# A one-core decoder step: a rotation's second half, a sample's start and a weight load move along the stream of input projections

## The chip, the cores and the metric

The kernel runs on one core of a Trainium2 chip. Its time is the device time of one execution in microseconds; shorter is better. TensorE (PE) multiplies matrices, VectorE (DVE) and ScalarE (ACT) work element by element, GpSimd (POOL) does a little of that and issues DMAs, SyncE (SP) only issues DMAs. Each takes its instructions in a fixed order and waits on semaphores for the others.

## The reference

One inference step of a single decoder layer, for a prompt of 1024 tokens and 8 samples of 4 tokens, all in float32 with D_MODEL 1024. Cut to what matters here:

```python
xn = rms_norm(x, g_pre_mix)
h = xn @ w_in            # [q_a|k_a|v_a|q_r|k_r|v_r|gate_r|gm_a|gm_r], 5888 columns
qr = rope_ret(q_r); kr = rope_ret(k_r) * DK_R ** -0.5
   # rope_ret(x) = x * cos + rot * sin, rot = stack([-x[1::2], x[0::2]])
o_r, new_s = retention(qr, kr, v_r, state)       # 4 heads, chunks of 128 tokens
y_a = o_a @ w_a_proj
y_r = (silu(gate_r) * head_rms(o_r)) @ w_r_proj
x = x + rms_norm((sigmoid(gm_a) * y_a + sigmoid(gm_r) * y_r) @ w_o, g_post_mix)
x = x + rms_norm(conv_ffn(rms_norm(x, g_pre_ffn)), g_post_ffn)
```

The samples use the same layer, with a retention state for each of the 8 (state_ret) that is read, used and written back.

## The kernel before

Precision: each float32 operand is split into a high part (a rounding cast, ScalarE) and the rest (a subtraction, VectorE); a product is three matmuls, high by high, high by low, low by high (lines 255 to 257, in mm3).

The large products are done with seven block products instead of eight, by sums of blocks of the weights and of the activations. The names A11, A12, A22, S1 to S4 stand for these seven products, and for their splits of the weights.

The part that the change touches is the function stream. It computes 16 groups of two 128-column blocks of w_in: first four pairs of q_r and k_r (one for each head), then the ret_gate, the gm_a and the gm_r columns. Each group is done for two halves of the 1056 tokens (i is the group, j the half). A half is seven products of 12 matmuls each (128x264 outputs), in the order A11, S1, A22 of the half before, S2, A12, S4, S3. They gather in PSUM banks: A11 and A12 in the one named q0, S2, S3 and A22 in q1 (two buffers), S1 and S4 in q2. The results go to a tile named pair by copies (L927) and two additions: L950 adds bank q2, after S4, and L952 adds bank q1, after S3. S1 of the next half writes q2, so it waits for L950.

stream is a generator, and every product is a yield: adv(n) runs n products and leaves the rest for later, so that other work (the samples, the retention blocks) is written between products.

The weights of the group after are prepared by in_split, a generator too. It loads two raw tiles (w_raw, L819, issued by SP, 512 KB each), and then gives one split after another; each is a cast on ACT (L331) and a subtraction on DVE (L223, where nearly all of DVE's two-operand work is recorded, in the helper ew). One split needs a sum of both halves of the second raw tile (s1, out<-in "s<-w_raw"). While the samples run there are two buffers for raw tiles; behind them a third is added.

For q_r and k_r a rotation follows each half (post_qk). In its first step the neighbouring rows of pair are exchanged by four DMAs on SP into two tiles sh (L860). The second step, turned, does three DVE operations for each of q and k (pair times rcos, sh times rsin, their sum) and stores the result to qk_d (L868, POOL). The first step is run by flush, at S2 of the half after; the second is kept in the list LATER and taken from there.

The samples (the function sample, once for each of 4 heads) begin after adv(20). A sample loads its rotated q and k from qk_d (L1045, SP), copies them (L1050, ACT), multiplies them (L1057), masks (L1060, DVE) and splits them (L1063, L1064). Then, four times, two retention states are split (s0s; L228 on ACT, L223 on DVE), multiplied (L1078), and updated (L1083 on PE, L1084 on DVE), and the new state is stored (L1086, POOL). At the end comes a norm over DVE (L1090), ACT (L1017, L1019, L1022) and POOL (L1021), and two transposes (L1028). s0s has one buffer, the raw states four.

The kernel is written with a framework that orders the instructions itself: a scheduler takes those that are ready by its own estimate of times, and prefers what the program has earlier. So a line that moves in the program can change the order of all engines around it. Semaphores and waits come from the framework.

Of the kernel before, what the change touches and what calls it, by code (L numbers as in the profile page):

```python
# [107 lines left out]
A11, A12, A22, S1, S2, S3, S4 = range(7)  # L108
# [12 lines left out]
def trunk(ctx, tc, I, O):  # L121
# [49 lines left out]
    def TT(name, shape=(P, T), dt=F32):  # L171
        return tpool.tile(list(shape), dt, name=name, tag="T")
# [17 lines left out]
    def psum(pl, tag, dt=F32):  # L190
        return pl.tile([P, 512], dt, name="ps_" + tag, tag=tag)
# [598 lines left out]
    ORDER = [0, 1, 2, 3, 4, 5, 8, 6, 9, 7, 10, 11, 12, 13, 14, 15]  # L790
# [108 lines left out]
    PEND, LATER = [], []  # L899

    def stream():

        ws = in_split(ORDER[0])
        next(ws)
        next(ws)
        ops = {p: next(ws) for p in EARLY[:5]}
        coming = in_split(ORDER[1])
        next(coming)
        last, nh = None, 0
        for i, n in enumerate(ORDER):  # L910
            for j in range(2):
                o = TT("pair")
                c11, c12, c21, c22 = (o[:, HW * q:HW * q + HW] for q in range(4))
                dst = {A12: c11, S1: c22, S2: c12, A22: c21}
                bk = [psum(pq, "q%d" % b)[:, :HW] for b in (0, 2)]
                b1 = pq.tile([P, 512], F32, name="ps_q1", tag="q1", bufs=2)[:, :HW]
                bk.insert(1, b1)
                if j:
                    nxt = {}

                def product(p, ps, t, j, dst):
                    for k in range(4):
                        xh, xl = xop(ex1, p, j, k)
                        mm3(ps, t[:, k], t[:, 4 + k], xh, xl, p in (A11, S1) and k == 0, k == 3,
                            skip_group_check=p not in (A11, S1))
                    if p in dst:
                        S.copy(out=dst[p], in_=ps)  # L927

                for p in (A11, S1, A22, S2, A12, S4, S3):
                    if p == A22:  # L930
                        if last is not None:
                            product(A22, *last)
                        if j == 0 and i:
                            ops[A22] = next(ws)
                            ws = coming
                            if i + 1 < len(ORDER):
                                next(ws)
                        if last is not None:
                            yield
                        continue  # L940
                    if p == S2:
                        if nh < 2:
                            TE.matmul(bk[1], ops[p][:, 0], xop(ex1, p, j, 0)[0], start=True, stop=True)
                            S.copy(out=bk[1], in_=bk[0])
                        nh += 1
                    product(p, bk[{A11: 0, A12: 0, S2: 1, S3: 1, S1: 2, S4: 2}[p]], ops[p], j, dst)
                    if p == A11 and nh >= 2:
                        S.copy(out=bk[1], in_=bk[0])
                    if p == S4:
                        V.tensor_tensor(out=c12, in0=bk[2], in1=c12, op=add)  # L950
                    if p == S3:
                        V.tensor_tensor(out=c22, in0=bk[1], in1=c22, op=add)  # L952
                    if p == S2:
                        flush()
                    if p == S1 and LATER:
                        LATER.pop()()
                    if p == S4 and S3 not in ops:
                        ops[S3] = next(ws)
                    if p == S3 and A22 not in ops:
                        ops[A22] = next(ws)  # L960
                        ws = coming
                        next(ws)
                    if j and i + 1 < len(ORDER):
                        nxt[p] = next(ws)
                        if p == S4 and i + 2 < len(ORDER):
                            coming = in_split(ORDER[i + 2])
                            next(coming)
                    yield
                last = bk[1], ops[A22], j, dst
                PEND.append(POST[n](j, o))  # L970
            if i + 1 < len(ORDER):
                ops = nxt
        product(A22, *last)
        flush()
        yield
# [3 lines left out]
    def adv(n):  # L979
        for _ in range(n):  # L980
            next(STR, None)

    def flush():
        while PEND:
            PEND.pop(0)()
# [108 lines left out]
    turns = []  # L1094
    for n in range(2):
        load_s0(n)
    adv(20)
    for h in range(4):
        for n, _ in enumerate(sample(h)):
            adv(3 if n < 4 else 2)  # L1100
# [30 lines left out]
    zlast, gts, qks, vts, state, quads, NBLK = [], {}, {}, {}, {}, {}, 4 * NB  # L1131
# [117 lines left out]
    coming, behind = ahead(0), None  # L1249
    for g in range(NBLK):  # L1250
        f, coming = coming, ahead(g + 1)
# [8 lines left out]
        behind = (g,) + m  # L1260
    adv(1)
    tail(*behind)
    adv(len(ORDER) * 14 - 8 - 82 - 4 * NBLK - 1)
    for n in range(4):
        load_z(n, quarters(ST("zt", (P, T), bufs=3)) if n < 2 else TT("z_raw", (P, 4, HW)))
    for _ in STR:
# [459 lines left out]
    ws = [products(S4, 1, pt, (1,), (0,)) for pt in range(3)]  # L1726
# [63 lines left out]
```

## Time and profile before

| | us |
|---|---|
| median of 3 runs | 1656.74 (1656.53 to 1758.46) |
| the profiled execution, its own time | 1658.69 |
| its span | 1656.9 |
| PE busy | 1626.7 |
| DVE busy | 1205.9 |
| ACT busy | 863.6 |
| POOL busy | 446.3 |

The profile is of one execution. Its times count from the first instruction. A row of a timeline is start, duration, engine, line, operation, out<-in, and in brackets the idle time of the engine before it and what ended that. In an entry of the waits, "PE ps_q L255 <- DVE pair L950: 3.1, 2, 2.1" means that PE waited at line 255, writing ps_q, for VectorE's instruction of line 950: 3.1 us in total, 2 times, 2.1 us the longest. The buffer numbers are left out in the profile's names. A matmul's record overlaps the next one; in an undisturbed stretch one starts every 0.12 us.

### The profile page before, as it was taken

Reading aid. Unit: us, or ns where it says so; the run is one execution under the profiler, and the core shown is the slowest. Engines: PE = TensorE matmul, PEld = TensorE weight load, DVE = VectorE, ACT = ScalarE, POOL = GpSimd, SP = SyncE. Lnnn points to the kernel's source line nnn. Section 1 sums busy time; section 2 is a strip of 40 time slices with the busy share of each in tenths; the row PEclk is TensorE's granted clock in tenths of the full one; section 3 lists DMA queues with packets and bytes.
Section 4 is the critical chain, followed back from the end, with each engine's and each line's share of the span. In section 5 each row is a group of like instructions: output and inputs, shape, how many; then the busy total and the mean of one; then the engine's idle time right before and its main releaser. Section 6 shows DMA issues by size and latency. Waiting matters only on the chain.

```text
span 1656.9 us, 32509 instructions
## 1 busy us (share of the span) xinstructions
PE 1626.7 (98%) x12551; PEld 1589.6 (96%) x12551; DVE 1205.9 (73%) x2035; ACT 863.6 (52%) x1882; POOL 446.3 (27%) x654
## 2 busy tenths in 40 slices
PE   8999999999999999999999999999999999999997
PEld 7999999999999999999789999999999999999997
DVE  7878749688565655569748988988988988445476
ACT  6565634456565655564424655555555556443343
POOL 4232431012233332243312422321231322111111
PEclk9999999999999999999999999999999999999999
DMA  7212235556677665697422245454545548766664
GB/s 201 65 49 71 72 80 193 185 187 191 207 230 235 197 216 156 209 309 234 157 89 89 59 148 173 161 162 160 182 136 177 173 150 253 237 196 198 194 186 145
DMA packets 275852, 278.22 MB, mean 168 GB/s; under 512 B 23552, under 2 KB 234784, under 8 KB 275681
## 3 DMA queue, kind: packets, MB, share of 16 engines
q1 hardware_dynamic: 241937, 159.58, 33.2%
q0 software_dynamic: 33760, 116.57, 20.1%
q8 instruction: 98, 1.61, 0.4%
q14 instruction: 57, 0.47, 0.1%
HBM read 184.24 MB, written 87.49 MB: 164 GB/s over the span
## 4 chain that ended last, share of the span: by engine, by line
PE 71%; DMA 3%; DVE 1%; issue 1%; ACT 0%; POOL 0%; DVEq 0%; POOLq 0%; SPq 0%
PE ps_m L255 10%; PE ps_m L257 10%; PE ps_m L256 10%; PE ps_t L256 8%; PE ps_t L255 8%; PE ps_t L257 8%; PE ps_q L255 4%; PE ps_q L257 4%; PE ps_q L256 4%; PE ps_b L1177 1%; PE ps_a L1181 1%; PE ps_b L1179 1%; DMA w_raw<-in_w_in 1%; DMA t<-in_w_o 1%; DMA vt<-v_d 0%
## 5 line engine op out<-in xcount | busy, mean ns | idle before, releaser
L255 PE MATMUL ps_t<-xh,w_hi 128*128 128x264 f32 (+2 forms) x524 | 148.9, 284 | 0.0
L223 DVE SCALAR_TENSOR_TENSOR w_lo<-w_raw,w_hi 128x1024 fp32r<-128x1024 f32 x82 | 103.6, 1268 | 62.0 <-ACT w_hi L228 57.2
L256 PE MATMUL ps_t<-xl,w_hi 128*128 128x264 f32 (+2 forms) x524 | 148.7, 284 | 0.0
L257 PE MATMUL ps_t<-xh,w_lo 128*128 128x264 f32 (+2 forms) x524 | 148.0, 283 | 0.0
L257 PE MATMUL ps_m<-xh,w_lo 128*128 128x264 f32 x512 | 145.4, 284 | 0.6 <-DVE w_lo L223 0.6
L255 PE MATMUL ps_m<-xh,w_hi 128*128 128x264 f32 x512 | 145.8, 285 | 0.0
L256 PE MATMUL ps_m<-xl,w_hi 128*128 128x264 f32 x512 | 145.4, 284 | 0.0
L223 DVE SCALAR_TENSOR_TENSOR w<-w_raw,w 128x512 fp32r<-128x512 f32 x152 | 104.2, 685 | 38.4 <-ACT w L331 38.0
L1537 DVE SCALAR_TENSOR_TENSOR c_out<-u_ext,fconst,c_out 128x1024 f32<-128x1024 f32 x96 | 121.9, 1280 | 2.1 <-ACT c_out L1533 0.3
L255 PE MATMUL ps_q<-xh,w 128*128 128x264 f32 x384 | 114.2, 297 | 3.1 <-DVE pair L950 3.1
L255 PE MATMUL ps_q<-ex,w 128*128 128x264 f32 x384 | 114.0, 297 | 0.6 <-DVE pair L952 0.6
L228 ACT CAST w_hi<-w_raw 128x1024 fp32r<-128x1024 f32 x62 | 65.2, 1052 | 92.7 <-PE ps_t L256 80.0
L256 PE MATMUL ps_q<-ex,w 128*128 128x264 f32 x384 | 110.6, 288 | 0.0
L256 PE MATMUL ps_q<-xl,w 128*128 128x264 f32 x384 | 110.5, 288 | 0.0
L257 PE MATMUL ps_q<-xh,w 128*128 128x264 f32 x384 | 110.4, 288 | 0.0
L257 PE MATMUL ps_q<-ex,w 128*128 128x264 f32 x384 | 109.8, 287 | 0.0
L331 ACT CAST w<-w_raw 128x512 fp32r<-128x512 f32 x152 | 94.7, 623 | 15.7 <-PE ps_q L257 8.2
L257 PEld LDWEIGHTS ps_t<-xh,w_lo 128*128 128x128 f32 x524 | 98.7, 188 | 0.0
L256 PEld LDWEIGHTS ps_t<-xl,w_hi 128*128 128x128 f32 x524 | 98.6, 188 | 0.0
L255 PEld LDWEIGHTS ps_t<-xh,w_hi 128*128 128x128 f32 x524 | 98.6, 188 | 0.0
L257 PEld LDWEIGHTS ps_m<-xh,w_lo 128*128 128x128 f32 x512 | 96.3, 188 | 0.8 <-DVE w_lo L223 0.8
L255 PEld LDWEIGHTS ps_m<-xh,w_hi 128*128 128x128 f32 x512 | 96.2, 188 | 0.0
(450 smaller groups left out, 6072.6 us busy)
## 6 DMA issues: line engine op xcount, KB each, us to landing
w_raw<-in_w_up SPq DMA_DIRECT2D x48, 512.0 KB, 4.3
w_raw<-in_w_in SPq DMA_DIRECT2D x42, 512.0 KB, 4.2
w_raw<-s_d SPq DMA_DIRECT2D x60, 256.0 KB, 4.1
t_d<-t POOLq DMA_DIRECT2D x24, 528.0 KB, 4.0
t<-t_d POOLq DMA_DIRECT2D x24, 528.0 KB, 4.9
t<-in_w_down SPq DMA_DIRECT2D x48, 256.0 KB, 5.2
s_d<-t POOLq DMA_DIRECT2D x24, 512.0 KB, 3.6
w_raw<-in_w_down SPq DMA_DIRECT2D x36, 256.0 KB, 5.1
```

The source lines that it names most:

```text
L223: pinned(V.scalar_tensor_tensor(out=out, in0=in0, scalar=1.0, in1=in1, op0=mult, op1=op))
L228: pinned(S.copy(out=hi, in_=src))
L255: TE.matmul(ps, wh, xh, start=start, stop=False, **kw)
L256: TE.matmul(ps, wh, xl, start=False, stop=False, **kw)
L257: TE.matmul(ps, wl, xh, start=False, stop=stop, **kw)
L331: S.copy(out=t[:, 0:4], in_=src)
L1177: TE.matmul(po, sT, vt, start=True, stop=tt == 0)
L1179: TE.matmul(po, q, state["s"], start=False, stop=True)
L1181: TE.matmul(pk, kt, vt, start=True, stop=True)
L1537: V.scalar_tensor_tensor(out=c[:, NS:], in0=u[:, g, NU + t:NU + t + SEQ], scalar=sc[t], in1=c[:, NS:], op0=mult, op1=add)
```

## The change

Three things move; what is computed stays.

The rotation's second step: the closure in LATER was run behind product S1, five products after the exchange was issued. It is now run at S2, seven products after it, just ahead of the flush that issues the next exchange.

The samples: they begin after 22 products of the stream instead of 20 and stay two products later; the count of products that run behind the retention blocks is two smaller.

The second raw tile: the generator's second step (the load of the second raw tile for the group after next) was taken at A22 of the next group's first half, behind the split of A22. It is now taken behind the split of S3, in the second half of the group before, three products earlier.

```diff
@@ stream, in the branch of product A22 @@
                         if j == 0 and i:
                             ops[A22] = next(ws)
                             ws = coming
-                            if i + 1 < len(ORDER):
-                                next(ws)
@@ stream, behind a product @@
                     if p == S2:
+                        if LATER:
+                            LATER.pop()()
                         flush()
-                    if p == S1 and LATER:
-                        LATER.pop()()
...
                     if j and i + 1 < len(ORDER):
                         nxt[p] = next(ws)
+                        if p == S3 and i + 2 < len(ORDER):
+                            next(coming)
                         if p == S4 and i + 2 < len(ORDER):
                             coming = in_split(ORDER[i + 2])
                             next(coming)
@@ the samples @@
-    adv(20)
+    adv(22)
@@ behind the retention blocks @@
-    adv(len(ORDER) * 14 - 8 - 82 - 4 * NBLK - 1)
+    adv(len(ORDER) * 14 - 8 - 84 - 4 * NBLK - 1)
```

The lines 950 and 952 of the kernel before are 948 and 950 of the changed one. Three places show what the scheduler makes of it; the numbers in the names tell tiles of one name apart, and differ between the two kernels.

VectorE, during the first sample. Here pair_3955 is the tile of the second group's second half, and pair_4133 (before) or pair_4116 (now) that of the half behind it. Before:

```order
L1084 SCALAR_TENSOR_TENSOR s0_3678<-s0_3678,ps_a_4197 128x512
L223 SCALAR_TENSOR_TENSOR pair_3955<-pair_3955,rcos_3663 128x528
L223 SCALAR_TENSOR_TENSOR sh_4220<-sh_4220,rsin_3664 128x528
L223 SCALAR_TENSOR_TENSOR s0s_4253<-s0_4115,s0s_4253 128x512
L950 TENSOR_TENSOR pair_4133<-ps_q2_4135,pair_4133 128x264
L223 SCALAR_TENSOR_TENSOR pair_3955<-pair_3955,sh_4220 128x528
```

And now:

```order
L223 SCALAR_TENSOR_TENSOR s0s_4222<-s0_3678,s0s_4222 128x512
L948 TENSOR_TENSOR pair_4116<-ps_q2_4118,pair_4116 128x264
L223 SCALAR_TENSOR_TENSOR pair_3955<-pair_3955,rcos_3663 128x528
L223 SCALAR_TENSOR_TENSOR sh_4202<-sh_4202,rsin_3664 128x528
L223 SCALAR_TENSOR_TENSOR s1_4281<-w_raw_4114 128x512
L950 TENSOR_TENSOR pair_4116<-ps_q1_4119,pair_4116 128x264
L1084 SCALAR_TENSOR_TENSOR s0_3678<-s0_3678,ps_a_4229 128x512
L223 SCALAR_TENSOR_TENSOR pair_3955<-pair_3955,sh_4202 128x528
L223 SCALAR_TENSOR_TENSOR w_raw_4114<-w_raw_4069,w_raw_4114 128x512
L223 SCALAR_TENSOR_TENSOR s0s_4287<-s0_4147,s0s_4287 128x512
```

The addition of bank q2 has moved from behind the first operations of this rotation to ahead of them. The states s0_4115 (before) and s0_4147 (now) are the same, the third pair of the first sample; their split has moved from two rows behind the rotation's first to seven behind it.

VectorE, as the third sample ends. s1 is the sum of the second raw tile, pair_5206 and pair_5186 the tile of the half that ends here. Before:

```order
L223 SCALAR_TENSOR_TENSOR s0s_5190<-s0_4969,s0s_5190 128x512
L223 SCALAR_TENSOR_TENSOR s1_5359<-w_raw_5252 128x512
L950 TENSOR_TENSOR pair_5206<-ps_q2_5208,pair_5206 128x264
L223 SCALAR_TENSOR_TENSOR w_raw_5252<-w_raw_5165,w_raw_5252 128x512
L1060 TENSOR_TENSOR t8_5123<-ps_a_5120,dm_5106 128x128
```

And now:

```order
L223 SCALAR_TENSOR_TENSOR s0s_5222<-s0_5003,s0s_5222 128x512
L948 TENSOR_TENSOR pair_5186<-ps_q2_5188,pair_5186 128x264
L223 SCALAR_TENSOR_TENSOR s1_5343<-w_raw_5184 128x512
L223 SCALAR_TENSOR_TENSOR w_raw_5184<-w_raw_5128,w_raw_5184 128x512
L950 TENSOR_TENSOR pair_5186<-ps_q1_5189,pair_5186 128x264
```

The addition of bank q2 and the sum s1 have changed places.

SyncE, around the loads of the first two samples (qk). Before:

```order
L1045 DMA qk_4038<-qk_d 128x2x32
L860 DMA sh<-pair 64x528 x2
L1043 DMA dm<-in_dmask 128x128
L860 DMA sh<-pair 64x528 x2
L1045 DMA qk_4394<-qk_d 128x2x32
L819 DMA w_raw<-in_w_in 128x8x128
L860 DMA sh<-pair 64x528 x2
```

And now:

```order
L1045 DMA qk_4073<-qk_d 128x2x32
L860 DMA sh<-pair 64x528 x4
L1043 DMA dm<-in_dmask 128x128
L1045 DMA qk_4429<-qk_d 128x2x32
L819 DMA w_raw<-in_w_in 128x8x128
L860 DMA sh<-pair 64x528 x2
```

The mask dm is loaded two exchange transfers later; the second sample's load stands in the same place, between the first and the last two transfers of one half's exchange. On TensorE (not shown) the first sample's first matmul, L1057, has moved from the 2289th to the 2307th place.

## The prediction

> **What bounds the kernel now.** I read the page first, then the waits of TensorE over the whole program, then its timeline at each wait, then the windows with the granted clock, and last VectorE's and SyncE's timelines behind the waits.
>
> ```profile
> span 1656.9 us, 32509 instructions
> PE 1626.7 (98%) x12551; PEld 1589.6 (96%) x12551; DVE 1205.9 (73%) x2035; ACT 863.6 (52%) x1882; POOL 446.3 (27%) x654
> ```
>
> TensorE bounds the kernel. Its busy time leaves 1656.9 - 1626.7 = 30.2 us in which it stands still, and the change removes no matmul. It can only gain from these 30 us, and from what standing still does to the clock. The part that the change touches is the stream of input projections, from about 290 to 700 us. TensorE's waits there, from the list of its waits (us in total, times, longest):
>
> ```profile
> PE ps_q L255 <- DVE pair L950: 3.1, 2, 2.1
> PE ps_b L1078 <- DVE s0s L223: 2.1, 1, 2.1
> PE ps_b L1028 <- ACT o L1022: 1.5, 1, 1.5
> PE ps_b L1177 <- DVE sT L1167: 0.7, 1, 0.7
> PE ps_q L255 <- DVE pair L952: 0.6, 1, 0.6
> PE ps_a L1057 <- ACT r L1050: 0.6, 1, 0.6
> ```
>
> The timeline of TensorE gives their places; in brackets stand the idle time and what ended it:
>
> ```profile
> 329.64 0.49 PE L1057 MATMUL ps_a<-r 128*128 128x128 f32 x2 [0.58 <-ACT r L1050]
> 336.34 0.39 PE L255 MATMUL ps_q<-xh,w 128*128 128x264 f32 x1 [0.98 <-DVE pair L950]
> 351.02 0.56 PE L1078 MATMUL ps_b<-s0s,q 128*64 128x256 f32 x3 [2.09 <-DVE s0s L223]
> 395.93 0.30 PE L1028 MATMUL ps_b<-ident,o 32*128 32x32 f32 x2 [1.50 <-ACT o L1022]
> 426.63 0.39 PE L255 MATMUL ps_q<-xh,w 128*128 128x264 f32 x1 [2.08 <-DVE pair L950]
> ```
>
> I call them W1 to W5. All lie in the stretch in which samples and rotations run beside the stream; together 0.58 + 0.98 + 2.09 + 1.50 + 2.08 = 7.2 us. The windows show that two of them cost more than their idle time (columns: width, then busy time and instructions of PE, PEld, DVE, ACT and POOL, then clock, DMA share, GB/s):
>
> ```profile
> 300.00:320.00 20.00, 20.00 (x166) 20.00 (x166) 16.01 (x26) 10.89 (x22) 1.26 (x2) 1.00 0.64 210
> 340.00:360.00 20.00, 17.91 (x136) 17.67 (x136) 15.38 (x28) 8.98 (x26) 3.58 (x5) 0.91 0.66 216
> 420.00:440.00 20.00, 17.92 (x135) 17.66 (x134) 10.77 (x21) 11.02 (x29) 2.76 (x4) 0.91 0.43 148
> 460.00:700.00 240.00, 239.33 (x1839) 234.25 (x1838) 139.54 (x297) 138.86 (x339) 83.97 (x141) 1.00 0.64 204
> ```
>
> An undisturbed window holds 166 matmuls, one per 20 / 166 = 0.120 us. The windows of W3 and W5 hold 30 and 31 fewer, 3.6 and 3.7 us, of which 2.1 is the wait. The other 1.5 to 1.6 us is the clock, 0.91 over these windows and 1.00 beside them. So waits of 2.08 and 2.09 us lowered the clock and one of 1.50 (W4) did not. The whole stretch has 7.2 + 1.5 + 1.6 = 10.3 us to give. After 460 us TensorE is idle for 0.67 us in 240: nothing is to be had there, only to be lost.
>
> [...]
>
> **The change part by part.** VectorE takes its instructions in order, so I look at what stands ahead of what TensorE waits for. Its timeline before:
>
> ```profile
> 326.87 0.71 DVE L223 SCALAR_TENSOR_TENSOR pair<-pair,rcos 128x528 f32<-128x528 f32 x1 [3.90 <-DMA sh<-pair]
> 333.22 0.28 DVE L1060 TENSOR_TENSOR t<-ps_a,dm 128x128 f32<-128x128 f32 x1
> 335.86 0.43 DVE L950 TENSOR_TENSOR pair<-ps_q,pair 128x264 f32<-128x264 f32 x1
> 349.03 0.71 DVE L223 SCALAR_TENSOR_TENSOR pair<-pair,rcos 128x528 f32<-128x528 f32 x1 [4.56 <-DMA sh<-pair]
> 350.28 0.68 DVE L223 SCALAR_TENSOR_TENSOR s0s<-s,s0s 128x512 fp32r<-128x512 f32 x1
> 362.10 0.41 DVE L950 TENSOR_TENSOR pair<-ps_q,pair 128x264 f32<-128x264 f32 x1
> 419.60 0.69 DVE L223 SCALAR_TENSOR_TENSOR s0s<-s,s0s 128x512 fp32r<-128x512 f32 x1
> 425.54 0.69 DVE L223 SCALAR_TENSOR_TENSOR s<-w_raw 128x512 f32<-128x512 f32 x1 [5.25 <-DMA w_raw<-in_w_in]
> 426.15 0.42 DVE L950 TENSOR_TENSOR pair<-ps_q,pair 128x264 f32<-128x264 f32 x1
> ```
>
> Samples two products later: the sample's first matmul (L1057) moves 18 matmuls back, 18 x 0.120 = 2.2 us, more than W1's 0.58: W1 goes. But W2 stands 44 matmuls further on, behind the same VectorE work as before: the 3.90 us stall at 326.87 keeps its place in VectorE's order, since the rotation there is not moved past anything, and only one sample operation, the 0.28 us of L1060 at 333.22, drops from ahead of the add at 335.86 to behind it. I take 0.2 us of it, since neighbours overlap by some 0.1 (none to all: 0 to 0.28). TensorE comes 0.6 us earlier and waits that much longer. W1 and W2 together: **-0.2** (-0.3 to 0).
>
> The rotation two products later: at 349.03 the rotation held the sample's split (350.28) behind an exchange that landed late. In the new order the next product's add (now L948) and the split before stand ahead of this rotation; the split that TensorE needs next stands seven instructions behind it instead of two. The exchange itself is not issued earlier, because it stands behind a sample's load on SyncE's queue (its wait in total, times and longest; then its timeline):
>
> ```profile
> SPq L1045 <- DMA qk_d<-pair: 13.7, 4, 5.2
> 342.78 0.37 SPq L1045 DMA_DIRECT2D qk<-qk_d  x1
> 343.79 1.18 SPq L860 DMA_DIRECT2D sh<-pair  x2
> ```
>
> In the new order that load still stands ahead of it: queued behind it are a weight load and the two transfers for which the rotation waits, and the matmuls that need the weights and the split wait for those. So the rotation still starts near 348.5. The split then starts seven steps of some 0.57 us later, at 352.5 (between 349.03 and 350.28 lie two steps of 0.62; the add's is shorter), and is done 0.7 us after that, at 353.2. TensorE's matmul that needs it moves 30 back in TensorE's order (number 2434 becomes 2464), which is 132 behind the one of W2. That one runs at 336.1, so TensorE is there at 336.1 + 132 x 0.120 = 352.0, and at 352.6 if it loses 0.6 us before, which I allow because ScalarE has a copy of the sample's load (L1050) ahead of the split before. So 0.6 and 0.6, 1.2 us of wait, in two pieces, each under the 1.50 that left the clock alone. W3 with its clock was 3.6: **-2.4** (-3.6 to 0).
>
> What is late next: VectorE itself is no earlier. The add at 362.10 is done at 362.51, and TensorE's first matmul that needs its bank came here:
>
> ```profile
> 363.99 0.29 PE L255 MATMUL ps_q<-xh,w 128*128 128x264 f32 x1
> ```
>
> The slack is 1.48 us. TensorE now comes 0.2 + 2.4 = 2.6 us earlier, and in the new order that add (the next L948) stands behind all three steps of a rotation whose exchange I put no earlier than before, so I let it end up to 0.9 us later: a wait of 1.1 to 2.0 us, and with the clock 3.6. I take **+2.0** (0 to +3.6).
>
> W4 waits for a chain over four engines, the longest of it on GpSimd:
>
> ```profile
> 392.90 2.44 POOL L1021 TENSOR_TENSOR rs<-ms,mhalf 32x1 f32<-32x1 f32 x1 [2.00 <-ACT ms L1019]
> 395.37 0.51 ACT L1022 ACTIVATE o<-t,rs 32x256 f32<-32x256 f32 x1 [2.56 <-POOL rs L1021]
> ```
>
> The transposes stand 51 matmuls behind the sample's last product, 50 before, and the chain is the same: **0** (-1.5 to +1.5).
>
> The second raw tile: while only two raw buffers exist, the load still has to wait for the split that frees its buffer; the new place in the program changes only what the scheduler puts around it. At W5 that is what matters: the sum that waits for the tile (425.54) stood ahead of the add (426.15), and in the new order the add stands ahead of the sum, right behind the split at 419.60. It can run near 420.3, and TensorE would need it only at 426.63 - 2.08 = 424.5. What is late next are the splits behind the sum: their first matmul comes about 80 later, 10 us, while the sum runs by about 425.5. W5 and its clock: **-3.7** (-3.7 to 0). After the samples there are three raw buffers and the load goes out some three products earlier; TensorE is busy there, so this is worth 0.
>
> Reordering elsewhere: every engine's order up to about 700 us is dealt anew. The nearest rows are the two small waits there, L1177 with 0.7 and L255 behind L952 with 0.6: they can go (-1.3), or one like W5 can appear (+3.7). I take **+1.3**, as much again as there is.
>
> Sum: -0.2 - 2.4 + 2.0 + 0 - 3.7 + 1.3 = -3.0 us. The profiled execution took 1658.7 us, its span being 1656.9; it would take 1655.7. The median of the runs, 1656.74, is 2.0 under the profiled one, so I forecast **1653.7**.
>
> [...]
>
> **The rivals.**
>
> All five waits go: 1656.7 - 10.3 = 1646.4. For it: the waits on the exchange were TensorE's largest. Against it: the 3.90 us stall ahead of W2 stays, and VectorE is 1.5 us ahead of TensorE at 363.99.
>
> Slower, because the adds behind the rotations take over: four more halves follow in which an add of S4's bank stands behind a rotation waiting for its exchange. A wait of 2.1 us in any of them halves the clock and costs 3.6. With two of them instead of my +2.0 the sum is -3.0 - 2.0 + 7.2 = +2.2, with three +5.8: 1659 to 1662.5. It decides from two such waits over about 2 us. For it: SyncE's queue blocks on stores of samples and of rotated tiles alike. Against it: the adds mostly moved ahead of the rotation that waits.
>
> [...]
>
> **How the numbers follow.** The forecast (1651 to 1656) gets 0.47, all five gone 0.15, the slower case 0.23, no change 0.15, of which the page's rule has 0.03. The 8-in-10 range reaches from 1647, leaving out half of the second case, to 1660.5, leaving out the worse half of the third. What a measurement of this kernel tells from no change is about 2%, 33 us. All idle time of TensorE is 30 us and the stretch has 10.3 with its clock, so faster by 2% gets 0.01; slower by 2% would take nine waits like W5, 0.02; within 2% 0.97.
>
> **What would show it.** In the changed kernel's profile: no wait of L1057 behind L1050; W2 still there, 1 to 1.7 us; no wait of L1078 behind the split over 1.5 us; a wait of L255 behind L948 near 363; none near 426, and the window there at clock 1.00. The forecast is wrong if L948 shows waits of 2 us or more in two halves, if W5 remains, or if waits appear after 460 us.

## The result

The changed kernel takes 1671.98 us (median of 6 runs, 1668.48 to 1673.0), the kernel before 1656.8 in the same comparison. The ratio is 1.0093, with a 95% interval of 1.0081 to 1.0104: the change costs 15.2 us, 0.9%. That is less than 2%, but far outside the interval of no change, and above the whole range that was forecast (1647.0 to 1660.5, with 1653.7 as the likeliest). The profiled execution took 1673.0 us, its span being 1671.2.

The page of the changed kernel:

```profile
span 1671.2 us, 32502 instructions
PE 1629.5 (98%) x12551; PEld 1590.6 (95%) x12551; DVE 1208.7 (72%) x2035; ACT 861.9 (52%) x1882; POOL 456.6 (27%) x654
```

The matmuls are the same in number, and the other engines have nearly the same to do. TensorE stands still for 1671.2 - 1629.5 = 41.7 us instead of 30.2. Its waits in the stretch of the samples (300 to 448 us; us in total, times, longest):

```profile
PE ps_q L255 <- DVE pair L950: 4.2, 2, 2.7
PE ps_q L255 <- DVE pair L948: 3.4, 4, 1.4
PE ps_q L255 <- ACT pair L927: 0.7, 1, 0.7
```

and from 690 to 800 us, where the stream ends and the output projection runs:

```profile
PE ps_m L255 <- DVE Gr L1302: 2.7, 1, 2.7
PE ps_t L255 <- DVE Gr L1304: 2.3, 2, 1.4
PE ps_q L255 <- DVE pair L950: 2.3, 2, 1.6
PE ps_m L255 <- DVE Gr L1304: 1.2, 1, 1.2
```

The second list is new. Before, TensorE waited there for 0.61 us behind a stream addition and for 0.57 behind a w_lo split; L1300 to L1306 are VectorE's additions that empty the projection's banks, and they were never late. One more new wait stands between the two stretches, in TensorE's timeline:

```profile
462.43 0.55 PE L1164 MATMUL ps_a<-qk 128*128 128x128 f32 x1 [2.59 <-DMA qk<-qk_d]
```

The windows show the clock at the three places where it fell (20 us each; the columns are those of the windows in the prediction):

```profile
420.00:440.00 20.00, 17.29 (x129) 16.90 (x128) 11.30 (x22) 10.92 (x28) 2.77 (x4) 0.91 0.44 146
460.00:480.00 20.00, 17.57 (x121) 17.14 (x122) 10.92 (x23) 8.31 (x23) 4.54 (x7) 0.91 0.98 295
780.00:800.00 20.00, 14.71 (x102) 13.89 (x102) 20.00 (x33) 7.36 (x15) 5.33 (x4) 0.91 0.72 221
```

To add up by place, I count matmuls: both kernels issue 12551, so the start of the n-th in one trace minus the start of the n-th in the other says how far behind the kernel is at that point of the work. (Some matmuls stand a few dozen places off in the other kernel, so a single point is good to some 0.5 us; and each trace is one execution.) With the kernel before as zero, the changed kernel gains or loses

| stretch, up to matmul | time before, us | change, us |
|---|---|---|
| samples, 3200 | to 448.1 | -0.2 |
| start of the retention, 3600 | to 501.4 | +3.4 |
| rest of the retention, 5000 | to 683.8 | 0.0 |
| end of the stream and first half of the output projection, 5700 | to 769.8 | +2.9 |
| second half of the output projection, 5800 | to 782.9 | +8.6 |
| all the rest, 12550 | to 1647.0 | -0.5 |
| together | | +14.3 |

The stretch of which the prediction speaks comes out even in this execution; nearly all the loss lies behind it. (The first row differs much between executions, as is shown below. The steps at the retention's start and in the second half of the projection are steadier: with the counts alone they are 3.0 and 8.3.) So two questions: what moved the later stretches, and where the gain in the samples went.

**What TensorE waits for near 780.** VectorE's timeline there, first to last:

```profile
762.34 1.23 DVE L223 SCALAR_TENSOR_TENSOR w_lo<-w_raw,w_hi 128x1024 fp32r<-128x1024 f32 x1 [4.13 <-ACT w_hi L228]
770.66 2.33 DVE L223 SCALAR_TENSOR_TENSOR w_loT<-t,w_hiT 128x1024 fp32r<-128x1024 f32 x1 [1.25 <-ACT w_hiT L228]
776.92 1.23 DVE L223 SCALAR_TENSOR_TENSOR w_loT<-t,w_hiT 128x1024 fp32r<-128x1024 f32 x1 [2.11 <-ACT w_hiT L228]
784.29 4.02 DVE L223 SCALAR_TENSOR_TENSOR xl<-Gr,xh 128x264 fp32r<-128x264 f32 x5
788.24 0.42 DVE L1302 TENSOR_TENSOR Gr<-ps_m,Gr 128x264 f32<-128x264 f32 x1
```

VectorE loses 4.13 + 1.25 + 2.11 = 7.5 us to splits that ScalarE, which casts first, hasn't begun in time. In the kernel before, its longest wait from 735 to 790 us was 1.02 us. ScalarE waits once for a matmul and twice for transfers:

```profile
761.26 1.05 ACT L228 CAST w_hi<-w_raw 128x1024 fp32r<-128x1024 f32 x1 [5.86 <-PE ps_t L257]
...
769.58 1.05 ACT L228 CAST w_hiT<-t 128x1024 fp32r<-128x1024 f32 x1 [3.38 <-DMA t<-in_w_o]
...
775.83 1.05 ACT L228 CAST w_hiT<-t 128x1024 fp32r<-128x1024 f32 x1 [4.25 <-DMA t<-in_w_o]
```

From 777 on VectorE runs without a break, and the additions come late, because they stand behind the splits in its order. The loads of w_o go out on SyncE's queue, the first of them at 739.5 us instead of 722.9. The order on that queue is another one from 685 us on (start, us from the first to the last of a group). Before:

```profile
682.60 1.04 SPq L316 DMA_DIRECT2D w_raw<-in_w_r_proj  x2
683.73 1.04 SPq L1228 DMA_DIRECT2D zt<-z_d  x2
...
689.06 1.67 SPq L316 DMA_DIRECT2D w_raw<-in_w_r_proj  x2
690.77 0.69 SPq L1287 DMA_DIRECT2D g_in<-gm_d  x1
...
698.61 5.84 SPq L316 DMA_DIRECT2D w_raw<-in_w_r_proj  x4
```

and now:

```profile
685.43 6.84 SPq L316 DMA_DIRECT2D w_raw<-in_w_r_proj  x3
692.32 1.08 SPq L1228 DMA_DIRECT2D zt<-z_d  x2
...
695.29 10.01 SPq L316 DMA_DIRECT2D w_raw<-in_w_r_proj  x3
705.35 0.57 SPq L1287 DMA_DIRECT2D g_in<-gm_d  x1
...
711.15 4.36 SPq L316 DMA_DIRECT2D w_raw<-in_w_r_proj  x2
```

Each weight tile is two loads. Before, two tiles (four loads) went out, then three pairs of gate tiles (g_in, a_in, 264 KB each), then tiles three and four. Now half of the second tile stands ahead of the z loads, and the whole third tile ahead of the gates. SyncE's waits from 690 to 715 us:

```profile
SPq L316 <- DVE w_lo L223: 7.7, 1, 7.7
```

The third tile's first load waits these 7.7 us for a buffer, and the six gate loads behind it wait with it. They start 14.6 us later than before (705.35 against 690.77), of which 3.2 are the kernel being behind as a whole. Then 1.6 MB of gates and the weights come at once. How this delay is handed on from there to 760 us isn't traced here; the experiments below change its beginning.

### The profile page after: what moved, and what is told of

Same layout as the page of the kernel before. It is cut to its first block, busy times and chain, and to the rows that moved or that the text cites. A ratio compares the mean times of both kernels' runs of the same rounds, so it can differ in the third digit from the quotient of the medians.

```text
span 1671.2 us, 32502 instructions
## 1 busy us (share of the span) xinstructions
PE 1629.5 (98%) x12551; PEld 1590.6 (95%) x12551; DVE 1208.7 (72%) x2035; ACT 861.9 (52%) x1882; POOL 456.6 (27%) x654
## 4 chain that ended last, share of the span: by engine, by line
PE 71%; DMA 3%; DVE 2%; issue 1%; ACT 0%; SPq 0%; POOL 0%; DVEq 0%; POOLq 0%; ACTq 0%
PE ps_m L255 10%; PE ps_m L257 10%; PE ps_m L256 10%; PE ps_t L256 8%; PE ps_t L255 8%; PE ps_t L257 8%; PE ps_q L255 4%; PE ps_q L256 4%; PE ps_q L257 4%; DMA qk<-qk_d 1%; PE ps_b L1177 1%; PE ps_a L1181 1%; PE ps_b L1179 1%; DVE xl L223 1%; DMA zt<-z_d 0%
## 5 line engine op out<-in xcount | busy, mean ns | idle before, releaser
L331 ACT CAST w<-w_raw 128x512 fp32r<-128x512 f32 x152 | 94.6, 622 | 14.3 <-PE ps_q L257 6.5
```

What stands on the lines that cost most here:

```text
L331: S.copy(out=t[:, 0:4], in_=src)
```

## The experiments

The change has three parts: the rotation, the raw load, the two counts. The counts, which the change names after the samples, also set where the retention begins. Nothing that follows moves, so the retention runs two products later against the stream as well. The first four kernels take these apart.

**The rotation alone.** From the kernel before, only this:

```diff
                     if p == S2:
+                        if LATER:
+                            LATER.pop()()
                         flush()
-                    if p == S1 and LATER:
-                        LATER.pop()()
```

> Only the rotation's second step is moved (from behind S1 to S2, ahead of the flush); samples, retention and raw loads stay. The change as a whole cost 15.2 us (1671.98 against 1656.8). Theory A, the loss comes from the products that the retention is moved back with the samples: nothing after 460 us changes, 1652 to 1659. Theory B, the rotation's new place makes the adds behind it late: 1662 or more, with waits of L948 of 2 us. Theory C, the second raw load's new place reorders SyncE's queue: as theory A here.

1655.57 us against 1657.49, ratio 0.9989 (0.9979 to 0.9998). TensorE has no wait over 0.65 us from 460 to 800, as theory A has it. But this is no second kernel. Its trace has the 32509 instructions of the kernel before, in the same order on all five engines, and the two programs are the same but for the numbers in tile names and of source lines. The line has moved; the scheduler's order has not. The same holds wherever only the rotation's place differs: for the raw load with and without it, for both mends with and without it (all below), and for the changed kernel itself. So theory B falls for want of any effect, and this run doesn't test theory A. The 0.11%, whose interval just misses 1, is a difference that two groups of runs of one program show. The waits in the samples' stretch are those of a second execution of the kernel before:

```profile
PE ps_q L255 <- DVE pair L950: 2.4, 3, 1.4
PE ps_b L1028 <- ACT o L1022: 2.1, 2, 1.1
PE ps_b L1078 <- DVE s0s L223: 1.3, 1, 1.3
```

W3 is 1.3 us here and was 2.09, W5 is 0.24 and was 2.08, and the clock did not drop (its mean over the execution is 0.998, in the profile before 0.996): this execution is 3.9 us ahead by matmul count at 448 us. So W3 and W5, from which the prediction took its largest gains, have no fixed size; a profile shows one draw from a range.

**The raw load alone.**

```diff
                             ops[A22] = next(ws)
                             ws = coming
-                            if i + 1 < len(ORDER):
-                                next(ws)
...
                         nxt[p] = next(ws)
+                        if p == S3 and i + 2 < len(ORDER):
+                            next(coming)
```

> Only the second raw weight tile's load is moved (from the next chunk's A22 to S3 of this one); rotation, samples and retention stay. Theory C (raw loads ahead of the retention's and the gates' loads on SyncE's queue): a wait of L1164 behind the qk load near 460 us, and 1661 or more. Theories A and B: 1654 to 1660, no wait over 1 us after 460.

1656.16 against 1657.49, 0.9994 (0.9983 to 1.0005). No change; theory C falls. Up to 559 us all engines have the order of the kernel before, so among the samples this move does nothing either. W5 is still there with 1.99 us (TensorE's timeline, 427.61): the raw load, to which the prediction gave W5's end, doesn't end it.

**The counts alone.**

```diff
-    adv(20)
+    adv(22)
...
-    adv(len(ORDER) * 14 - 8 - 82 - 4 * NBLK - 1)
+    adv(len(ORDER) * 14 - 8 - 84 - 4 * NBLK - 1)
```

> Only the two counts are changed (22 for 20, 84 for 82): samples and, with them, the whole retention run two products later against the stream; rotation and raw load stay. Theory A: the loss is here, 1666 to 1674, with most of the waits of the output projection (L1300 to L1306, near 750 to 790 us, some 7 us with a clock drop). Theories B and C: 1654 to 1660, and that stage waits under 1 us as before.

1673.0 against 1657.49, 1.0094 (1.0079 to 1.0109). The whole loss is here; by matmul count 8.3 us of it in the second half of the projection, as in the changed kernel. So is the new order: TensorE, ScalarE and GpSimd have the changed kernel's from end to end, VectorE and SyncE up to 462 us (of what follows, three and two of their instructions stand elsewhere). The three places shown ahead of the prediction are thus the work of the counts; rotation and raw load have no part in them.

**All but the retention.** The changed kernel, with the retention back in its place:

```diff
-    adv(2)
+    adv(0)
     turns.pop()()
...
-    adv(len(ORDER) * 14 - 8 - 84 - 4 * NBLK - 1)
+    adv(len(ORDER) * 14 - 8 - 82 - 4 * NBLK - 1)
```

> The changed kernel, but the retention stays in its old place in the stream: the two products that the samples are later are taken from the two between the last sample and the retention (0 for 2), and the last count is 82 as before. Theory A: the waits near 700 and 750 to 790 us go, 1652 to 1660. Theories B and C: 1666 to 1674, since rotation and raw load are as in the changed kernel.

1666.23 against 1657.49, 1.0053 (1.0038 to 1.0068): between the two forecasts. The projection is clean again; from 690 to 800 us TensorE waits only as it did before:

```profile
PE ps_q L255 <- DVE pair L950: 0.6, 1, 0.6
PE ps_m L257 <- DVE w_lo L223: 0.6, 1, 0.6
```

So the 11.5 us behind 684 belong to the retention's two products. But 2.7 us are lost among the samples and 6.5 at the retention's start, where the wait for qk stays (2.66). The samples' own delay costs there. The retention now starts right behind the last sample, and its start loses 6.5 us instead of 3.4, so the parts don't add up: 0.53% here and 0.69% for the next kernel, but 0.93% together.

**The retention alone.** The kernel before with only the retention two products later:

```diff
-    adv(2)
+    adv(4)
     turns.pop()()
...
-    adv(len(ORDER) * 14 - 8 - 82 - 4 * NBLK - 1)
+    adv(len(ORDER) * 14 - 8 - 84 - 4 * NBLK - 1)
```

> The kernel before, with only the retention two products later against the stream (4 for 2 products between the last sample and the retention, 84 for 82 at the end); samples, rotation and raw load stay. Theory A (the retention's end has lost its lead over the output projection, whose loads then collide): waits of L1300 to L1306 near 750 to 790 us of some 5 to 9 us in all, no wait behind a qk load near 460, 1662 to 1668. Rival (these waits need the new order of the samples as well): 1655 to 1660.

1667.51 against 1656.19, 1.0069 (1.0052 to 1.0085). No wait for qk, and the projection waits as in the changed kernel (in TensorE's timeline):

```profile
776.68 0.39 PE L255 MATMUL ps_m<-xh,w_hi 128*128 128x264 f32 x1 [1.20 <-DVE Gr L1304]
...
783.66 0.36 PE L255 MATMUL ps_m<-xh,w_hi 128*128 128x264 f32 x1 [2.66 <-DVE Gr L1302]
```

Two ways are left: the retention's end has lost lead over the projection, or the scheduler's new order of SyncE's queue does it. Three kernels tell them apart.

**One product instead of two**, by 3 for 2 and 83 for 82:

> The kernel before with the retention one product later (3 for 2 behind the last sample, 83 for 82 at the end); two products alone cost 11.3 us. In this order too the third weight tile stands ahead of the gate loads. If the order on the queue decides: 1663 to 1668, nearly as much as two. If the lead decides, in proportion: 1660 to 1663. If it is a threshold that one product doesn't pass: 1655 to 1658.

1664.13 against 1655.47, 1.005 (1.0035 to 1.0065). The second half of the projection loses 7.4 us, as much as with two products. In the queue the z loads have their old place, but tiles two and three stand ahead of the gates:

```profile
687.57 10.40 SPq L316 DMA_DIRECT2D w_raw<-in_w_r_proj  x4
698.01 0.57 SPq L1287 DMA_DIRECT2D g_in<-gm_d  x1
```

**Four products**, by 6 for 2 and 86 for 82:

> The kernel before with the retention four products later (6 for 2, 86 for 82). If the lead decides, in proportion: 1675 to 1682. If the order on the queue decides: 1663 to 1670, as two products (1667.5). If the gain is back with another order: under 1660.

1665.48 against 1655.47, 1.0055 (1.004 to 1.007), with 4.5 us in the second half of the projection. With 1, 2 and 4 products that stretch loses 7.4, 7.4 and 4.5 us: not in proportion to the lead.

**The gates first.** The changed kernel; the first three pairs of gates are requested ahead of the projection's loop, and the third weight tile is held behind them on the queue:

```diff
+    for m in range(3):
+        gates[m, 0], gl = gate_in(m, 0)
     wnext = z_weights(0)
...
-                wnext = z_weights(2 * pi + c + 1)
+                if 2 * pi + c + 1 in (2,):
+                    with tc.issue_after(gl.ins):
+                        wnext = z_weights(2 * pi + c + 1)
+                else:
+                    wnext = z_weights(2 * pi + c + 1)
```

(gate_in holds the two loads that merge did, and merge takes these tiles for its first three calls.)

> The changed kernel, with the first three pairs of gate loads (L1287) held ahead of the third tile of output-projection weights on SyncE's queue, as they stood in the kernel before; nothing else. In the changed kernel that tile's first half stood ahead of them and waited 7.8 us for a buffer (L316, 704.37). If this head of the queue makes the gates and the weights collide after 705 us, the waits of L1302 and L1304 near 778 to 790 shrink to under 2 us: 1663 to 1667. If the two products of lead themselves are what is missing, they stay: 1670 to 1674.

1666.78 against 1655.47, 1.0068 (1.0051 to 1.0085), where the changed kernel has 1.0093. TensorE's order is that of the changed kernel but for two matmuls near 722 us, yet the waits at the projection's banks are gone. The queue, where the gates (now L1286) go out 7.5 us earlier, and the window:

```profile
697.03 0.75 SPq L316 DMA_DIRECT2D w_raw<-in_w_r_proj  x1
697.83 2.51 SPq L1286 DMA_DIRECT2D g_in<-gm_d  x1
...
705.79 6.21 SPq L316 DMA_DIRECT2D w_raw<-in_w_r_proj  x4
```

```profile
775.00:795.00 20.00, 19.44 (x158) 19.17 (x157) 20.00 (x35) 5.45 (x10) 3.64 (x3) 1.00 0.70 213
```

By count the second half of the projection now costs -0.1 instead of +8.6. The runs show less of it, 0.25% or some 4 us between the two ratios, and this profile was the fastest of its runs. The retention still ends two products later here, so the lead is not the cause; the order that the scheduler deals is. Both profiles with both mends, below, repeat the -0.1. Not shown apart is how that order acts: with the gates first, VectorE and ScalarE too have another order between 711 and 763 us, so that late transfers are the likely way but not the only one left.

**One gate pair.** The changed kernel with less to stand in the weights' way:

```diff
-    gpool = pool("apool", 3, stack=ph_stack)
+    gpool = pool("apool", 1, stack=ph_stack)
```

> The changed kernel, with one buffer instead of three for the pairs of gate tiles (g_in, a_in, L1287): of the six early gate loads that stand ahead of the output projection's weights on SyncE's queue two are left. If the waits of L1302 and L1304 near 778 to 790 us come from weights that land late behind these transfers, they shrink by more than half: 1662 to 1667. If they come from elsewhere: 1671 to 1674; if single buffers make GpSimd's products late: more.

1674.73 against 1656.19, 1.0117 (1.0102 to 1.0132). The projection's second half loses 3.9 us instead of 8.6, as expected if transfers collide; but a wait of 1.78 us behind L1302 at 786.93 is left, and past the projection come two of 2.42 and 2.71 us behind o_t. Another 5.5 us are lost there, presumably because with a single buffer the later gates come late. It speaks for the collision and is no mend.

**The wait for qk near 462 us.** Queues before, SyncE then GpSimd:

```profile
446.16 3.55 SPq L1138 DMA_DIRECT2D qk<-qk_d  x5
452.03 0.36 SPq L1154 DMA_DIRECT2D z<-gr_d  x1
448.29 0.57 POOL L1107 DMA_DIRECT2D out_k_sample<-in_cache_k  x1
```

and now:

```profile
452.52 0.37 SPq L1154 DMA_DIRECT2D z<-gr_d  x1
452.93 5.37 SPq L1138 DMA_DIRECT2D qk<-qk_d  x5
450.20 0.57 POOL L1107 DMA_DIRECT2D out_k_sample<-in_cache_k  x1
```

Two things are different: the gate load (z), which waited 5.6 us for the store of gr_d that it reads (not for a free tile, as the next expectation has it), is ahead of the qk loads, and the two cache copies, which GpSimd starts when the last sample is done, are ahead of them too. One kernel for each.

*The order.* The changed kernel, with the first five qk loads and the first z load held in the order of the program:

```diff
-        ld.dma_start(out=qks[g], in_=qk_d[h].rearrange("i p t -> p i t")[:, :, cols(tt)])
+        q_in = ld.dma_start(out=qks[g], in_=qk_d[h].rearrange("i p t -> p i t")[:, :, cols(tt)])
+        if g < 5:
+            pin(q_in)
```

(and the same for the z load of head 0.)

> The changed kernel, with the first five qk loads of the retention held ahead of its first gate load (z) on SyncE's queue, the order of the kernel before. If the 2.6 us wait of L1164 behind the qk load near 462 us comes from standing behind the z load, which waits for a free tile, it goes with its clock drop: 4 us less, 1667 to 1669. If it comes from the transfers sharing the bandwidth, it stays: 1671 to 1673.

1677.66 against 1656.19, 1.0135 (1.012 to 1.015): some 7 us worse than the changed kernel (1.0093), which neither theory had. The loads go out at 447.8, and the wait for qk falls to 0.75 us. But the scheduler now puts the last sample's end and the retention's start differently, and TensorE waits for others:

```profile
451.26 0.42 PE L1028 MATMUL ps_b<-ident,o 32*128 32x32 f32 x2 [2.96 <-ACT o L1022]
...
464.20 0.49 PE L255 MATMUL ps_q<-ex,w 128*128 128x264 f32 x1 [2.73 <-DVE pair L950]
```

It says nothing against the order as a cause, but holding a load in place rearranges whatever stands around it.

*The copies.* The changed kernel; the loop that starts the two copies is moved into the retention's loop, at block 8:

```diff
     for g in range(NBLK):
+        if g == 8:
+            for nm in "kv":
+                pin(st.dma_start(out=O[nm + "_sample"][0].rearrange("b r k d -> b r (k d)")[:, 0:P - DS, :],
+                                 in_=I["cache_" + nm][0].rearrange("b r k d -> b r (k d)")[:, DS:P, :]))
```

> The changed kernel, with the two cache copies (L1107, from the inputs to out_k_sample and out_v_sample, on GpSimd's queue) issued eight blocks of the retention later. In the changed kernel they go out at 450.2 and the first qk loads at 452.9, behind them; before, the qk loads went first, at 446.2. If the copies' traffic makes the qk loads land late, the wait of L1164 near 462 goes with its clock drop: 1667 to 1669. If not: 1671 to 1673.

1671.64 against 1655.47, 1.0095 (1.0075 to 1.0115). The z load is still ahead of the qk loads (456.91 and 457.32), but the qk loads land in 5.4 us instead of 9.2, and there is no wait of TensorE from 460 to 480:

```profile
460.00:480.00 20.00, 20.00 (x161) 19.71 (x159) 12.74 (x25) 11.54 (x27) 4.46 (x7) 1.00 1.04 313
```

That the samples are later in this execution isn't the reason: with both mends (below), 1.2 us behind the kernel before at 448 us and, in the second kernel, 1.5 us ahead of it, TensorE doesn't wait for qk either. So the wait for qk comes from the copies' traffic. In what way copies started by GpSimd hold up loads started by SyncE was not shown. In the runs this mend alone shows nothing: their 8 us of spread (1667.46 to 1675.73) hide it, and in the profiled one the samples lost 4.3 us.

**Both mends.** The gates first and the copies later in one kernel:

> The changed kernel with both mends: the first three gate pairs ahead of the third weight tile, and the cache copies eight blocks later. By the profiles the one took 8.3 us off the output projection and the other 3.4 us off the wait near 462: 1672 - 11.7 = 1660, against 1656 before. If the stretch of the samples itself gained what the prediction said (4.3 us), it would be 1652 to 1654; if it costs nothing and gains nothing, 1656 to 1658; if it costs, 1659 to 1664.

1661.11 against 1654.78, ratio 1.0029 (1.0018 to 1.004). The two places behind the samples account for 0.93 - 0.29 = 0.64 points of the 0.93, some 10.6 of the 15.2 us. What is left, 0.29% or 4.8 us, is what the expectation calls a cost of the samples' stretch.

**Both mends, old rotation.** The same with the rotation behind S1:

> The same with both mends, but the rotation's second step in its old place behind S1. If moving the rotation is what gains in the samples' stretch (alone it took 4.1 us off it in one profile, 1.9 in the runs), this is 2 to 4 us slower than with it. If beside the later samples its place doesn't matter: within 1 us.

1660.29, 1.0029 (1.0019 to 1.0039). No difference, and there can be none: it is the same program as the kernel above.

**The two parts without the counts.**

> Rotation and second raw load as in the changed kernel, the counts as before (20 and 82). Rotation alone gave 1655.57, raw load alone 1656.16, before 1657.49. If the parts add: 1653.5 to 1655.5. If they disturb each other as the parts of the whole change did: over 1658.

1655.51 against 1656.19, 0.9999 (0.9989 to 1.0008): no change. It is the program of the raw load alone. Its execution has 4.3 us less among the samples and 3.5 more at the retention's start, where TensorE waits 1.99 us for sT and 1.5 us more are lost, as much as the clock drop at W3 cost; that of the raw load alone had 0.8 more and 0.3 less. The difference is one of executions.

**The rotation with later copies**, to see whether it beats both kernels:

> The kernel before with the rotation moved and the cache copies eight blocks later, nothing else. The rotation alone gave 1655.57 (0.9989). The wait of L1177 behind sT near 470 was 0.4 us there; if the copies' traffic costs the retention's start more than this wait shows, 1652 to 1655; if the copies get in the way later, over 1656.

1656.53 against 1654.78, 1.0003 (0.9994 to 1.0012). It doesn't. Since the rotation's move changes nothing, this is the kernel before with later copies. None of these kernels is faster than the kernel before; the 0.9989 above is that kernel measured twice.

**What the samples' stretch costs.** One profile says little here, since it differs between executions of the same order. Up to matmul 3200 (448 us) seven profiles have the order of the kernel before on all five engines (before, rotation alone, raw load alone, the two without the counts, rotation with later copies, retention later by one and by two). Eight have that of the changed kernel (changed, counts alone, all but the retention, one gate pair, gates first, copies later, both mends with either rotation). At that matmul they stand as follows against the profile before:

| order | us against the profile before | mean |
|---|---|---|
| of before | -4.3, -3.9, -2.5, -2.4, -1.2, 0, +0.8 | -1.9 |
| of the changed kernel | -1.5, -0.2, +0.4, +1.2, +1.3, +1.4, +2.7, +4.3 | +1.2 |

The new order costs about 3.1 us up to there (1 to 5 with 95%), and executions of one order scatter by 5 to 6 us. At 403 us (matmul 2860) the two means are 0.4 us apart and at 420 us 1.2, within the scatter. The rest comes at W5, where TensorE waits 2.13 us at most in the seven, in one of them less than 0.2, and 2.37 to 3.06 us in the eight. So the -0.2 of the changed kernel's profile is one of the better executions of an order that loses.

## Why the prediction was wrong

It forecast -3.0 us, and 15.2 came. Step by step:

**Samples two products later (-0.2).** This is the step that failed. W1 went as forecast; W2 was 0.43 us instead of 1 to 1.7, and 0.24 to 1.84 in the eight executions of this order. But the step took the counts for a matter of the samples and priced two matmuls of one sample. The same two numbers hold the retention two products back, and that was not priced at all: alone it costs 11.3 us. The place to see it was in the diff, where the last count changes from 82 to 84: everything between that line and the samples moves against the stream. And it isn't the lost lead itself that costs, but the order that the scheduler makes of it.

**Reordering elsewhere (+1.3, at most +3.7).** It was sized by the waits that TensorE had after 460 us before, 0.67 us in 240. But a wait that isn't there shows no size. What could be lost was the slack of the loads: for the qk load and at the projection's banks TensorE did not wait at all before. Measured: 3.4 us at the retention's start and 11.5 behind 684, by matmul count. That TensorE is idle for little there, "nothing is to be had there, only to be lost", was right, and its price was one wait like W5. Waits after 460 us stand in the prediction's own list of what would show it wrong.

**The rotation (-2.4, next +2.0).** The new order was put down to the wrong edit: it comes from the counts, and the rotation's move changes nothing. Of what the order does, a part was read rightly. L1078 no longer waits for the split, and the addition behind the rotation (L948) waited 1.20 us at 360.96, where 1.1 to 2.0 were forecast near 363. Not so the start: the exchange went out at 340.76 instead of 343.79, and the rotation began at 345.57, not near 348.5. And W3's place gains nothing, because the other bank was missed:

```profile
349.22 0.39 PE L255 MATMUL ps_q<-ex,w 128*128 128x264 f32 x1 [1.48 <-DVE pair L950]
```

That is the addition of q1, which stands behind a sum that waits for its raw tile. In the eight executions of the new order this wait is 1.08 to 2.28 us; L1078 had waited 1.05 to 2.27 in the seven of the old. One wait was exchanged for another of its size.

**W5 and the raw load (-3.7).** Half right. VectorE's timeline of the changed kernel:

```profile
420.46 0.43 DVE L948 TENSOR_TENSOR pair<-ps_q,pair 128x264 f32<-128x264 f32 x1
426.12 0.69 DVE L223 SCALAR_TENSOR_TENSOR s<-w_raw 128x512 f32<-128x512 f32 x1 [5.22 <-DMA w_raw<-in_w_in]
426.84 0.69 DVE L223 SCALAR_TENSOR_TENSOR w_raw<-w_raw 128x512 f32<-128x512 f32 x1
427.45 0.42 DVE L950 TENSOR_TENSOR pair<-ps_q,pair 128x264 f32<-128x264 f32 x1
```

The addition of q2 runs at 420.46, where 420.3 was forecast, and nobody waits for it. But the half has a second addition, of q1, and that one stayed behind the sum and its 5.22 us. TensorE waits for it, and the clock drops (0.50 from 428.19 to 431.60 us):

```profile
427.93 0.39 PE L255 MATMUL ps_q<-ex,w 128*128 128x264 f32 x1 [2.71 <-DVE pair L950]
```

"What is late next" was asked of the splits alone; the row of L950 behind the two sums stands in the order shown ahead of the prediction. Nor is it the raw load that moved q2's addition: it stands there with the counts alone, where TensorE waits 3.06 us at the same place, and with the raw load alone the order of W5 is the old one.

**W4 (0).** It went (no transpose of a sample waits more than 0.15 us there), a gain of 1.5 and the end of the range given.

**The slower rival** had the adds behind the rotations as its mechanism, from two waits over 2 us: 1659 to 1662.5. One wait of that size came, behind the other addition (2.71), and the mended kernel, where only this stretch is left, gives 1.0029, which would be 1661.5. So that rival has about the size of the samples' part, though not its mechanism. The rest no case had.

**No change (0.15).** No run shows the rule to which 0.03 of it goes. In the profile before, the waits of 2.09 and 2.08 us (W3, W5) were each followed by 3.41 us at a clock of 0.50.

Still open: how the 4.8 us that are left after both mends divide. The samples' order explains some 3.1 by profiles with much scatter, and 1.3 more lie at the end of the stream in the mended profile, where additions of the stream (L950) are late for a reason that wasn't looked into. Open too is what hands the delay on from SyncE's queue near 705 us to the additions near 780.

## What to carry to other kernels

Before a part of a change is given credit, compare its order on every engine with the one before: where a scheduler deals the order, a moved line can give the same program, and what is then measured is the scatter of the runs. A count that places one piece of work in a stream places all that follows it: go through the program behind the edit and ask of each later stage how much lead its loads have lost, and what is now ahead of them in their queue. Where a scheduler deals the order anew, compare the order of the load queue at every stage that changes, above all for a load that must wait for a buffer and now stands ahead of loads whose buffers are free. Engine idle time before the change, with what it cost in clock (7.2 and 3.1 us in the stretch of the samples here), bounds what can be gained, but not what can be lost.

## What the runs showed of the hardware

- The clock. In the seventeen profiles, past the first 100 us, none of 76 waits of TensorE between 0.9 and 1.5 us halved the granted clock (to 0.50), 13 of 25 between 1.5 and 2.0 did, and 26 of 35 between 2.0 and 3.1. 1.52 us was enough in one case, and 2.79 us was not in another; these 39 drops lasted 3.41 us (35) or 6.83 us (4). The prediction had taken 2 us for a threshold; in these profiles it is a chance, and it rises with the length (0, 52 and 74%). What decides it for a single wait was not shown.
- The same order of instructions gives times of one stretch that differ by 5 to 6 us between executions (the table of the samples' stretch). Waits differ from one to the next (W5 from under 0.2 to 2.13 us in seven of them), and with them whether the clock drops; why the waits differ wasn't looked into.
- In the changed kernel a load that waited 7.7 us for its buffer held back six others on its queue. With those six ahead of it, 8.6 us of TensorE's time some 80 us later were gone, in three profiles. In between TensorE lost little, and no wait in its list named the queue.
